# First products by slices of 2, 2, 4, 4, 4 blocks with six more pairs of partial sums, and six attention gates put into DRAM early

## The chip, the cores and the metric

The kernel runs on one core of one Trainium2 chip. The metric is the device time of one execution in microseconds. Three runs of the kernel before gave a median of 1566.24 us (1565.78 to 1566.56).

## The reference

One decoder block on x (256 tokens, width 2048, float32), conditioned on a vector c. What matters here:

```
mod = silu(c) @ w_ada + b_ada                      # 2048 x 12288: sh1, sc1, gt1, sh2, sc2, gt2
h = rms_norm(x, norm1_gain) * (1 + sc1) + sh1
p = h @ w_in + b_in                                # columns: r, k, v, LoRA inputs, q, ak, av, gates of both branches
y_rwkv = rwkv7_branch(p_rwkv, ...)                 # 16 heads of 64, a recurrence over the 256 tokens
y_attn = sliding_window_sink_attention(q, k, v, sinks)
merged = g_rwkv * (y_rwkv @ w_branch_rwkv) + g_attn * (y_attn @ w_branch_attn)
x = x + gt1 * (merged @ w_out)
x = x + gt2 * (relu(h2 @ w_up)**2 @ w_down)        # h2: rms_norm and sh2, sc2 again
return rms_norm(x, final_gain)
```

All weights are float32 and are read once. Products are made in three passes with a high and a low part of either operand.

## The kernel before

**Products.** A product keeps 128 x 128 blocks of weights as the stationary operand and streams the 256 tokens. `split` (L267) loads a piece of 1024 columns of weights (0.5 MB, tag `raw`, a ring of 7 buffers that the tiles of w_ada share), casts it to the high part on ScalarE (L274) and subtracts it for the low part on VectorE (L275). `feed` (L278) turns a piece into 24 products on TensorE (L297): high weights with high and low tokens, low weights with high tokens. `cols_product` (L303) is a product over the whole depth into one PSUM bank.

**Modulation and slices.** The first norm needs sh1 and sc1 for each block of 128 of the 2048 inputs. `modulated(part)` (L373) makes them for one slice of blocks (`SL`, L34): for the first slice with TensorE (`ada_pe`, L192), for the others with VectorE (`ada_dve`, L207, multiply-adds at L219). The loop at L948 goes over the slices. In each one it feeds the six kept banks (L955), which gather over all slices in PSUM (LoRA inputs, first keys, r, v, q, attention keys), and then the `sums` (L426): ten banks of 256 columns, two at a time, whose partial sums are taken out of PSUM after each slice, copied in the first one (L967) and added in SBUF in the others (L969). While a slice is fed, the modulation of the next one runs as a background job. In the last slice, after the fourth of the sums, `begin_heads` (L878) and `begin_attention` (L895) start the two branches.

**The order of the work.** Background jobs are generators. `pulse` (L253) is called after each piece and lets each queue take as many steps as its rate allows: `RATE_ADA` and `RATE_BG` for the rows of w_ada (`bg`), `RATE_ATT` for attention, `RATE_RW` for the RWKV branch. A step costs 1 credit, or what it yields: the steps of `chains` yield 0.5. The tile layer then orders the instructions on each engine and sets the waits; each engine works its list off in order, and SyncE issues nearly all DMAs, also in order.

**The RWKV branch** (`rwkv`, L771) works on four groups of heads, two at a time: `prep` (L480: decay, norm of the keys with the sums at L515, an inverse root on VectorE at L519 and its transposed copy at L537, and the triangular products at L566), `inverse16` (L608: the triangles go to DRAM at L573, are read back in another layout at L611, inverted in 30 steps on GpSimd at L619 and L621, written at L622 and L624 and read back at L629), `levels` (L636, from L644: the inverse is built up), `chains` (L675: the recurrence) and `norm` (L726). The second pair of groups needs the keys, r and v of `keyed` (L1002), which are products of their own at L1012; they go through DRAM.

**After the first products** come three gate products, the keys of the third group, those of the fourth, `gd2` (L996) and more gates. A gate of the RWKV branch is written to DRAM (`grd`) until it is used. Attention's gates are made just ahead of the branch product that uses them (L1029, L1032). `finish(rw)` at L1036 drains the RWKV branch before its own branch product (L1044).

Of the kernel before, what the change touches and what calls it, by code (L numbers as in the profile page):

```python
# [18 lines left out]
P = 128  # L19
# [12 lines left out]
NSUM = 4  # L32
NZ = 3
SL = (4, 4, 4, 4)  # L34

RATE_ADA = 1.5
RATE_RW = 1.2
RATE_ATT = 1.0
RATE_BG = (0.9, 0.3, 0.4, 0.2)
# [43 lines left out]
def hybrid_block(ctx: ExitStack, tc, x, c, w_ada, b_ada, norm1_gain, w_in, b_in, rwkv_mix, rwkv_w0,  # L83
# [194 lines left out]
    def feed(w, k0, nk, cols, blocks, xh, xl, begin, end, tw=T):  # L278


        width = sum(m for _, _, m in blocks)

        def load(raw, a, m):
            o = 0
            for c0, n in cols:
                nc.sync.dma_start(raw[:, :, o:o + n],
                                  w.rearrange("(kc p) n -> p kc n", p=P)[:, k0 + a:k0 + a + m, c0:c0 + n])
                o += n

        for a, n, hi, lo in split(nk, width, load):  # L290
            for wt, xs in ((hi, (xh, xl)), (lo, (xh,))):
                for kk in range(n):
                    k = k0 + a + kk
                    o = 0
                    for ps, j, m in blocks:
                        for xx in xs:
                            TE.matmul(ps[0:m, j * tw:(j + 1) * tw], lhsT=wt[:, kk, o:o + m], rhs=xx(k),  # L297
                                      start=(k == begin and xx is xh and wt is hi and j == 0),
                                      stop=(k == end and wt is lo), skip_group_check=True)
                        o += m  # L300
            pulse(0.5)
# [114 lines left out]
    def flat(t, g=0):  # L416
# [9 lines left out]
    sums = [(("k", 1), O_K + 256), (("r", 1), O_R + 256), (("v", 1), O_V + 256)] + \  # L426
           [(("q", i), O_Q + 256 * i) for i in range(1, 4)] + \
# [4 lines left out]
    rest = [(t_s1, 0), (t_s1, 1), (t_s2, 0), (t_s2, 1)] + rest  # L432

# [12 lines left out]
    sgd2 = kd[0:32, 0, :]  # L446
# [154 lines left out]
    def zero_inverses():  # L601
        z = arena[0][:, 2 * W3:2 * W3 + BP // 2]
        G.memset(z, 0.0)
        for n in range(2):
            for h in range(2):
                nc.sync.dma_start(scr2[n].rearrange("u (q e) -> (u q) e", q=4)[:, h * BP // 2:(h + 1) * BP // 2], z)
# [68 lines left out]
    def chains(sts, dds):  # L675
# [13 lines left out]
        for c in range(NCH):  # L689
# [11 lines left out]
            yield 0.5  # L701
# [8 lines left out]
            yield 0.5  # L710
# [11 lines left out]
            yield 0.5  # L722
# [79 lines left out]

    arena = [tl("a1", (8 * T,)), tl("a2", (8 * T,))]
# [67 lines left out]
    def pair(q2, qT=None):  # L871
        if qT is None:
            qT = qas[q2 % 2]
# [39 lines left out]
    for _ in range(8):  # L913
# [27 lines left out]
    def keys_out(ss, n, src):  # L941
# [4 lines left out]
        spilled.add((ss, n))  # L946

    for part, nk in enumerate(SL):  # L948
# [9 lines left out]
        for g2 in range(0, len(sums), 2):  # L958
            two = sums[g2:g2 + 2]
            ps = [ps_ax() for _ in two]  # L960
            feed(w_in, k0, nk, [(c, 256) for _, c in two], [(p, j, P) for p in ps for j in range(2)],
                 hA, hB, k0, k0 + nk - 1)
            for a, ((what, n), _) in enumerate(two):
                t, j = rest[g2 + a]
# [37 lines left out]
    def keyed(ss):  # L1002
        for n in range(3):
            keys_out(ss, n, cols_product(w_in, KC, (O_K, O_R, O_V)[n] + ss * 256, [P, P], hA, hB))
# [257 lines left out]
```

## Time and profile before

| | |
|---|---|
| median of 3 runs | 1566.24 us |
| profiled execution | 1566.93 us, span 1565.1 us |
| TensorE (PE) busy | 1510.9 us, 97% of the span |
| VectorE (DVE) busy | 1100.7 us, 70% |
| ScalarE (ACT) busy | 722.6 us, 46% |
| GpSimd (POOL) busy | 40.5 us, 3% |
| DMA | 372.8 MB, 238 GB/s on the mean |
| granted TensorE clock | 0.987 of full on the mean |

The profile is one execution, recorded by the hardware. Busy time is the union of an engine's instructions; TensorE's are pipelined, so the mean length of one product (286 ns) is longer than the distance to the next. Idle time in front of an instruction is shown in brackets with what ended it.

### The profile page before, as it was taken

The numbers are of one execution on the slowest core, as the hardware profiler recorded it, in microseconds if no ns is written. First come the engines' busy times: TensorE is split into PE (matmuls) and PEld (weight loads), VectorE is DVE, ScalarE is ACT, GpSimd is POOL, SyncE is SP. The second block draws the span as 40 slices with busy tenths as digits, with TensorE's granted clock in tenths as the row PEclk, the third lists the DMA queues.
The fourth block names the chain that finished last, engine by engine and source line by source line (L and its number), as shares of the span: only waits on it lengthen the run. The fifth ranks groups of instructions, "written<-read, shape, count | busy, mean of one in ns | idle before, by whom it ended". The sixth has DMA issues, their size and how long they took to land.

```text
span 1565.1 us, 30120 instructions
## 1 busy us (share of the span) xinstructions
PE 1510.9 (97%) x12122; PEld 1385.8 (89%) x12122; DVE 1100.7 (70%) x1784; ACT 722.6 (46%) x1107; POOL 40.5 (3%) x97
## 2 busy tenths in 40 slices
PE   5899999999999999999999999999999999999997
PEld 2898999889989898989889998989898898989985
DVE  1879979867789857669769755666666666555576
ACT  3353377655355433345447444434444343444443
POOL 2000000030000030000000000000000000000000
PEclk9899999999999999999999999999999999999999
DMA  9999978869888859849865777677776776566652
GB/s 343 335 325 295 342 234 245 245 170 310 283 262 285 269 155 297 282 147 339 285 215 173 240 222 228 216 222 226 225 228 211 227 222 205 184 188 189 194 183 81
DMA packets 297100, 372.80 MB, mean 238 GB/s; under 512 B 40912, under 2 KB 198384, under 8 KB 296320
## 3 DMA queue, kind: packets, MB, share of 16 engines
q1 hardware_dynamic: 296448, 370.72, 74.7%
q8 instruction: 95, 1.56, 0.4%
q0 software_dynamic: 512, 0.15, 0.1%
q14 instruction: 45, 0.37, 0.1%
HBM read 357.96 MB, written 12.86 MB: 237 GB/s over the span
## 4 chain that ended last, share of the span: by engine, by line
PE 87%; DVE 4%; DMA 3%; ACT 2%; issue 2%; POOL 1%; SPq 0%; POOLq 0%; DVEq 0%; ACTq 0%
PE mm L297 41%; PE mm L319 14%; PE ax L319 14%; PE ax L297 9%; PE ax L683 2%; PE ax L186 1%; PE ax L478 1%; DVE wlo L275 1%; DVE acc L219 1%; PE ax L566 1%; DMA ada<-in_w_ada_dram 1%; ACT whi L274 1%; DMA tt<-in_x_dram 1%; PE ax L653 0%; PE ax L237 0%
## 5 line engine op out<-in xcount | busy, mean ns | idle before, releaser
L274 ACT CAST whi<-raw 128x1024 fp32r<-128x1024 f32 x458 | 478.0, 1047 | 673.4 <-PE mm L297 257.0
L275 DVE TENSOR_TENSOR wlo<-raw,whi 128x1024 fp32r<-128x1024 f32 x458 | 557.0, 1219 | 267.3 <-ACT whi L274 258.6
L297 PE MATMUL mm<-h,whi 128*128 128x256 f32 (+1 forms) x3296 | 446.8, 286 | 3.4 <-ACT whi L274 3.4
L297 PEld LDWEIGHTS mm<-h,whi 128*128 128x128 f32 (+1 forms) x3296 | 415.2, 192 | 10.1 <-ACT whi L274 3.4
L219 DVE SCALAR_TENSOR_TENSOR acc<-ada,cact,acc 128x512 f32<-128x512 f32 x330 | 247.0, 749 | 60.2 <-DMA ada<-in_w_ada_dram 55.6
L297 PE MATMUL mm<-h,wlo 128*128 128x256 f32 (+1 forms) x1648 | 237.7, 284 | 0.0
L297 PEld LDWEIGHTS mm<-h,wlo 128*128 128x128 f32 (+1 forms) x1648 | 215.0, 191 | 1.1 <-issue 0.7
L319 PE MATMUL mm<-whi,u 128*128 128x512 f32 x512 | 138.3, 392 | 0.0
L319 PE MATMUL ax<-whi,u 128*128 128x512 f32 x512 | 138.0, 391 | 0.0
L297 PE MATMUL ax<-h,whi 128*128 128x256 f32 x768 | 109.0, 290 | 9.0 <-DVE p L969 4.5
L319 PEld LDWEIGHTS ax<-whi,u 128*128 128x128 f32 x512 | 96.2, 188 | 21.0
L319 PEld LDWEIGHTS mm<-whi,u 128*128 128x128 f32 x512 | 95.6, 188 | 20.2
L297 PEld LDWEIGHTS ax<-h,whi 128*128 128x128 f32 x768 | 100.2, 197 | 11.4 <-ACT whi L274 5.0
L319 PE MATMUL ax<-wlo,u 128*128 128x512 f32 x256 | 79.4, 391 | 0.0
L319 PE MATMUL mm<-wlo,u 128*128 128x512 f32 x256 | 79.3, 391 | 0.0
L297 PE MATMUL ax<-h,wlo 128*128 128x256 f32 x384 | 59.2, 287 | 0.0
L319 PEld LDWEIGHTS mm<-wlo,u 128*128 128x128 f32 x256 | 48.1, 188 | 10.5
L319 PEld LDWEIGHTS ax<-wlo,u 128*128 128x128 f32 x256 | 48.1, 188 | 10.5
L297 PEld LDWEIGHTS ax<-h,wlo 128*128 128x128 f32 x384 | 52.6, 197 | 0.1
L297 PE MATMUL mm<-tt,whi 128*128 128x256 f32 x256 | 37.7, 298 | 2.1 <-ACT tt L768 2.1
L297 PEld LDWEIGHTS mm<-tt,whi 128*128 128x128 f32 x256 | 34.5, 203 | 3.2 <-ACT tt L768 2.3
L319 PE MATMUL mm<-whi,m 128*128 128x512 f32 x128 | 35.0, 392 | 0.0
(345 smaller groups left out, 1489.1 us busy)
## 6 DMA issues: line engine op xcount, KB each, us to landing
ada<-in_w_ada_dram SPq DMA_DIRECT2D x192, 512.0 KB, 5.5
raw<-in_w_up_dram SPq DMA_DIRECT2D x128, 512.0 KB, 3.9
raw<-in_w_down_dram SPq DMA_DIRECT2D x128, 512.0 KB, 4.0
raw<-in_w_in_dram SPq DMA_DIRECT2D x72, 512.0 KB, 5.2
raw<-in_w_in_dram SPq DMA_DIRECT2D x128, 256.0 KB, 5.1
raw<-in_w_out_dram SPq DMA_DIRECT2D x32, 512.0 KB, 6.1
raw<-in_w_branch_attn_dram SPq DMA_DIRECT2D x16, 512.0 KB, 5.9
raw<-in_w_branch_rwkv_dram SPq DMA_DIRECT2D x16, 512.0 KB, 5.2
```

Source lines behind the costliest of these rows:

```text
L186: TE.matmul(ps[:, j:j + 1], lhsT=acc[:, j * P:(j + 1) * P], rhs=ones[:, 0:1], start=True, stop=True)
L219: V.scalar_tensor_tensor(o, in0=t[:, a, :], scalar=ck, in1=o, op0=ALU.mult, op1=ALU.add)
L274: S.copy(hi[:], raw[:])
L275: V.tensor_tensor(lo[:], raw[:], hi[:].bitcast(F32), op=ALU.subtract)
L297: TE.matmul(ps[0:m, j * tw:(j + 1) * tw], lhsT=wt[:, kk, o:o + m], rhs=xx(k), start=(k == begin and xx is xh and wt is hi and j == 0), sto ...
L319: TE.matmul(pss[tb][:], lhsT=uu(k)[:, sl], rhs=wt[:, kk, :], start=(first and k == 0), stop=(final and k == kblocks - 1))
L478: TE.matmul(out[hs, :], lhsT=src[hs, chunk(c)], rhs=ident[hs, hs], start=True, stop=True)
L566: TE.matmul(pT[hs, o:o + P], lhsT=src[hs, chunk(c)], rhs=ar[hs, i, c].rearrange("p a b -> p (a b)"), start=True, stop=True)
L683: TE.matmul(ps[hs, j, i, part, :], lhsT=lhs(j, i, hs), rhs=rhs(j, i, hs), start=(first and j == 0 and i == 0), stop=True, skip_group_check ...
```

## The change

The slices are 2, 2, 4, 4 and 4 blocks (`SL`), so the first products need the modulation of two blocks. The columns k, r and v of the third and fourth group of heads (`keys`) join the sums: 16 banks in place of ten; `keyed` is gone, and `keys_out` is called from the last slice. Four pairs, or one in a slice of 4 (`4 // nk`), are fed with one load of 0.5 MB, and with `apart` all products of one bank stand together. `begin_heads` is called after the third of the sums and `begin_attention` after the tenth, each with its own rate. The steps of `chains` cost 1 in place of 0.5, and the rates are 2.15 for RWKV (1.2 before), 1.35 for w_ada behind the first products (0.9) and 1.0 inside them (1.5). `gd2` and all RWKV gates follow the first products, then six attention gates, which go to DRAM (`grd` has 16 places), and two more are made where all eight were. In a slice of 2 blocks two pairs share a load.

```diff
-SL = (4, 4, 4, 4)
-
-RATE_ADA = 1.5
-RATE_RW = 1.2
+SL = (2, 2, 4, 4, 4)
+
+RATE_ADA = 1.0
+RATE_RW = 2.15
 RATE_ATT = 1.0
-RATE_BG = (0.9, 0.3, 0.4, 0.2)
+RATE_BG = (1.35, 0.3, 0.4, 0.2)
...
-    def feed(w, k0, nk, cols, blocks, xh, xl, begin, end, tw=T):
+    def feed(w, k0, nk, cols, blocks, xh, xl, begin, end, tw=T, apart=False):
...
+        groups = [[b for b in at if b[1] is ps] for _, ps, j, _ in at if j == 0] if apart else [at]
...
+            for group in groups:
+                for wt, xs in ((hi, (xh, xl)), (lo, (xh,))):
+                    for kk in range(n):
+                        k = k0 + a + kk
+                        for o, ps, j, m in group:
+                            for xx in xs:
+                                TE.matmul(ps[0:m, j * tw:(j + 1) * tw], lhsT=wt[:, kk, o:o + m], rhs=xx(k),
...
-    grd = tc.dram_tile([8, P, 2 * T], F32, name="grd")
+    grd = tc.dram_tile([16, P, 2 * T], F32, name="grd")
...
+    keys = [((n, ss), o + 256 * ss) for ss in (2, 3) for n, o in (("k", O_K), ("r", O_R), ("v", O_V))]
+    sums = [(("k", 1), O_K + 256), (("r", 1), O_R + 256), (("v", 1), O_V + 256)] + keys + [(("q", i), O_Q + 256 * i) for i in range(1, 4)] + \
            [(("g", g), O_GR + 256 * g) for g in range(NSUM)]
...
-    sgd2 = kd[0:32, 0, :]
+    sgd2 = mx.tile([32, T], F32, name="sgd2")
...
-            yield 0.5
+            yield
...
-                while len(spilled - {'gd2'}) < 7:
+                while not {w for w, _ in keys} <= spilled:
                     yield
...
-        for g2 in range(0, len(sums), 2):
-            two = sums[g2:g2 + 2]
-            ps = [ps_ax() for _ in two]
-            feed(w_in, k0, nk, [(c, 256) for _, c in two], [(p, j, P) for p in ps for j in range(2)],
-                 hA, hB, k0, k0 + nk - 1)
...
+        for g0 in range(0, len(sums), 4 // nk):
+            some = sums[g0:g0 + 4 // nk]
+            ps = [ps_ax() for _ in some]
+            feed(w_in, k0, nk, [(c, 256) for _, c in some], [(p, j, P) for p in ps for j in range(2)],
+                 hA, hB, k0, k0 + nk - 1, apart=True)
...
-            if last and g2 == 2:
-                finish(bg)
-                begin_heads()
-                begin_attention()
-                rate["rw"], rate["att"] = RATE_RW, RATE_ATT
+                    elif n > 1:
+                        keys_out(n, "krv".index(what), o)
+                    spilled.add((what, n))
+                    if (what, n) == ("v", 1):
+                        finish(bg)
+                        begin_heads()
+                        rate["rw"] = RATE_RW
+                    if (what, n) == ("q", 1):
+                        begin_attention()
+                        rate["att"] = RATE_ATT
...
+    def gates_late(g):
+        gate_out(8 + g, tl("gr", (2, T), 3), cols_product(w_in, KC, O_GA + g * 256, [P, P], hA, hB))
...
-    left = list(range(NSUM, 16))
-    for g in left[:3]:
+    gd2()
+    spilled.add("gd2")
+    for g in range(NSUM, 8):
         gates(g)
-    for ss in range(2, 4):
-        keyed(ss)
-        if ss == 3:
-            finish(att)
-            gd2()
-            spilled.add("gd2")
-    for g in left[3:8 - NSUM]:
-        gates(g)
+    for g in range(NLATE):
+        gates_late(g)
+    finish(att)
+    gates_late(NLATE)
...
-        gate_of(8 + g, t, cols_product(w_in, KC, O_GA + g * 256, [P, P], hA, hB))
+        if g <= NLATE:
+            nc.sync.dma_start(flat(t), grd[8 + g])
+        else:
+            gate_of(8 + g, t, cols_product(w_in, KC, O_GA + g * 256, [P, P], hA, hB))
```

Further, `zero_inverses` zeroes a smaller piece and writes it four times in place of twice, and the partial sums of the keys use the two attention tiles `a1` and `a2` before attention needs them.

Lines of the changed kernel that are named below: L303 is `feed`'s product (L297 before), L575 and L585 are in `prep` (L566, L576), L524 and L546 the norm of the keys (L515, L537), L653 the first product of `levels` (L644), L187 a column sum of w_ada (L186).

**The rates move the second inverse.** On TensorE, from the last triangular products of the second `prep` (L566) to the first products with the inverse (L644); `whi` is the high part of a piece of weights, `in` the inverse's data, `tt` the triangles. Each row of L297 below is the first one of a piece of 24 products. Before:

```order
L566 MATMUL ax_6819<-ar_6014,p_850_6520 64x128 x2
...
L297 MATMUL mm_7005<-a_719_5660,whi_7008 128x256
...
L297 MATMUL mm_7005<-a_719_5660,whi_7042 128x256
...
L297 MATMUL mm_7084<-h_218,whi_7087 128x256
...
L297 MATMUL mm_7084<-h_218,whi_7121 128x256
...
L297 MATMUL mm_7084<-h_219,whi_7196 128x256
...
L297 MATMUL mm_7084<-h_219,whi_7230 128x256
...
L297 MATMUL mm_7260<-a_719_5660,whi_7263 128x256
...
L297 MATMUL mm_7260<-a_719_5660,whi_7297 128x256
...
L297 MATMUL mm_7332<-h_218,whi_7335 128x256
...
L644 MATMUL ax_7375<-in_7074,tt_6286 64x64 x16
L644 MATMUL ax_7393<-in_7075,tt_6309 64x64 x16
```

And with the change:

```order
L575 MATMUL ax_6981<-ar_6334,p_898_6740 64x128 x2
...
L303 MATMUL mm_7161<-a_953_7133,whi_7164 128x256
L303 MATMUL mm_7287<-a_953_7133,whi_7290 128x256
...
L303 MATMUL mm_7161<-a_953_7133,whi_7251 128x256
...
L303 MATMUL mm_7287<-a_953_7133,whi_7324 128x256
...
L653 MATMUL ax_7360<-in_7123,tt_6544 64x64 x16
L653 MATMUL ax_7378<-in_7124,tt_6567 64x64
...
L653 MATMUL ax_7378<-in_7124,tt_6567 64x64 x15
```

Nine pieces of products stood between the two before, and four stand there now; the pieces with `a` are of the attention branch's product.

**The norm of the keys in the first pair of heads.** On TensorE, from the sums of squares (L515, into two `ax` banks) to the products with the inverse roots (`yn`, L537). Before, with the first rows of each piece and of the attention work between:

```order
L515 MATMUL ax_2767<-kt,p_358_2633 128x2 x2
L515 MATMUL ax_2794<-kt,p_367_2650 128x2 x2
L297 MATMUL ax_2828<-h_219,whi_2833 128x256
...
L297 MATMUL ax_2828<-h_219,whi_2864 128x256
...
L855 MATMUL ax_2893<-kt,a_50_248 128x128 x3
...
L297 MATMUL mm_2967<-h_218,whi_2970 128x256
...
L862 MATMUL ax_2892<-a_51_249,vtok 64x128
L864 MATMUL ax_2892<-a_51_249,vtok 64x128 x2
...
L855 MATMUL ax_2912<-kt,a_50_248 128x128 x3
...
L862 MATMUL ax_2911<-a_51_249,vtok 64x128
...
L537 MATMUL ax_2930<-kt,yn_2783 128x128 x2
L537 MATMUL ax_2944<-kt,yn_2810 128x128 x2
```

And with the change:

```order
L524 MATMUL ax_3239<-kt,p_435_3169 128x2 x2
L524 MATMUL ax_3266<-kt,p_444_3186 128x2 x2
L303 MATMUL ax_3301<-h_215,whi_3304 128x256
...
L303 MATMUL ax_3301<-h_215,wlo_3305 128x256 x8
L546 MATMUL ax_3332<-kt,yn_3255 128x128 x2
L546 MATMUL ax_3346<-kt,yn_3282 128x128 x2
```

One piece of 24 products is left in between; before there were more than two pieces and the steps of attention.

## Rows read from the trace of the kernel before

**Rows 1.** The page's busy times (busy, share of the span, instructions).

```profile
PE 1510.9 (97%) x12122; PEld 1385.8 (89%) x12122; DVE 1100.7 (70%) x1784; ACT 722.6 (46%) x1107; POOL 40.5 (3%) x97
```

**Rows 2.** TensorE's timeline at the start: begin, length (us), engine, line, what; idle before.

```profile
11.67 4.16 PE L200 MATMUL ax<-ada,in 128*32 128x512 f32 x12 [3.37 <-DMA ada<-in_w_ada_dram]
...
34.22 1.05 PE L200 MATMUL ax<-ada,in 128*32 128x512 f32 x4 [1.64 <-DMA ada<-in_w_ada_dram]
...
41.19 1.22 PE L297 MATMUL mm<-h,whi 128*128 128x256 f32 x4 [3.36 <-ACT whi L274]
```

**Rows 3.** A window of 50 us in the slices.

```profile
core 0: us, PE busy (x) PEld busy (x) DVE busy (x) ACT busy (x) POOL busy (x), PEclk, DMA share, GB/s
150.00:200.00 50.00, 47.42 (x391) 46.67 (x390) 46.50 (x64) 18.84 (x24) 0.00 (x0) 1.00 1.02 331
```

**Rows 4.** TensorE's timeline in the slices.

```profile
49.17 2.08 PE L297 MATMUL mm<-h,whi 128*128 128x256 f32 x16
51.09 1.12 PE L297 MATMUL mm<-h,wlo 128*128 128x256 f32 x8
...
132.20 0.95 PE L297 MATMUL ax<-h,whi 128*128 128x256 f32 x6 [1.35 <-DVE p L969]
...
139.20 1.05 PE L186 MATMUL ax<-kt,acc 128*128 128x1 f32 x8 [0.55 <-DVE tt L969]
...
190.60 1.05 PE L186 MATMUL ax<-kt,acc 128*128 128x1 f32 x8 [0.55 <-DVE tt L969]
```

**Rows 5.** VectorE by line, 100 to 200 us: busy, mean ns; idle before.

```profile
L219 DVE SCALAR_TENSOR_TENSOR acc<-ada,cact,acc 128x512 f32<-128x512 f32 x56 | 41.8, 749 | 1.0
L275 DVE TENSOR_TENSOR wlo<-raw,whi 128x1024 fp32r<-128x1024 f32 x32 | 38.6, 1219 | 1.2 <-ACT whi L274 1.1
...
L969 DVE TENSOR_TENSOR tt<-ax,tt 128x512 f32<-128x512 f32 x10 | 6.4, 686 | 0.9 <-PE ax L297 0.9
```

**Rows 6.** TensorE's timeline around the second inverse.

```profile
553.40 0.44 PE L566 MATMUL ax<-ar,p 64*64 64x128 f32 x4
...
586.64 0.30 PE L644 MATMUL ax<-in,tt 64*64 64x64 f32 x2 [0.80 <-DMA in<-scr]
589.12 1.99 PE L644 MATMUL ax<-in,tt 64*64 64x64 f32 x32 [2.19 <-DMA in<-scr]
592.26 1.97 PE L644 MATMUL ax<-in,tt 64*64 64x64 f32 x30 [1.15 <-DMA in<-scr]
```

**Rows 7.** SyncE's own queue at the second inverse.

```profile
554.61 1.25 SPq L573 DMA_DIRECT2D scr<-tt  x2
...
558.34 0.44 SPq L611 DMA_DIRECT2D lg<-scr  x1
...
582.24 7.43 SPq L629 DMA_DIRECT2D in<-scr  x8
```

**Rows 8.** GpSimd's timeline at both inverses.

```profile
346.06 0.63 POOL L623 COPY p<-p 128x256 f32<-128x256 f32 x1
...
563.53 0.47 POOL L619 TENSOR_TENSOR rs<-lg,p 128x15 f32<-128x15 f32 x1 [50.64 <-DMA lg<-scr]
...
579.16 0.63 POOL L623 COPY p<-p 128x256 f32<-128x256 f32 x1
```

**Rows 9.** TensorE's timeline around the first inverse.

```profile
319.22 0.44 PE L566 MATMUL ax<-ar,p 64*64 64x128 f32 x4
...
361.22 2.08 PE L644 MATMUL ax<-in,tt 64*64 64x64 f32 x64
```

**Rows 10.** TensorE's timeline at the last norm of the keys.

```profile
526.56 0.95 PE L515 MATMUL ax<-kt,p 128*128 128x2 f32 x8
...
539.79 0.71 PE L537 MATMUL ax<-kt,yn 128*128 128x128 f32 x4 [1.81 <-ACT yn L521]
```

**Rows 11.** Windows of 20 us behind two waits.

```profile
540.00:560.00 20.00, 20.00 (x241) 18.12 (x241) 15.87 (x32) 6.56 (x13) 0.00 (x0) 0.91 0.68 209
...
580.00:600.00 20.00, 15.86 (x214) 15.23 (x213) 8.59 (x13) 2.09 (x2) 0.00 (x0) 0.83 0.90 233
```

More of the change, by code (lines that the diff above doesn't have):

```diff
@@ L32 @@
 NSUM = 4
+NLATE = 5
 NZ = 3
-SL = (4, 4, 4, 4)
-RATE_ADA = 1.5
-RATE_RW = 1.2
+SL = (2, 2, 4, 4, 4)
+RATE_ADA = 1.0
+RATE_RW = 2.15
 RATE_ATT = 1.0
-RATE_BG = (0.9, 0.3, 0.4, 0.2)
+RATE_BG = (1.35, 0.3, 0.4, 0.2)
 RATE_Z = 2.0
@@ L276, in split @@
             yield a, m, hi, lo
-    def feed(w, k0, nk, cols, blocks, xh, xl, begin, end, tw=T):
+    def feed(w, k0, nk, cols, blocks, xh, xl, begin, end, tw=T, apart=False):
         width = sum(m for _, _, m in blocks)
+        at, o = [], 0
+        for ps, j, m in blocks:
+            at.append((o, ps, j, m))
+            o += m
+        groups = [[b for b in at if b[1] is ps] for _, ps, j, _ in at if j == 0] if apart else [at]
         def load(raw, a, m):
@@ L290, in feed @@
         for a, n, hi, lo in split(nk, width, load):
[L291 to L300, printed above, removed]
+            for group in groups:
[5 more added lines that the diff above has]
+                                TE.matmul(ps[0:m, j * tw:(j + 1) * tw], lhsT=wt[:, kk, o:o + m], rhs=xx(k),
+                                          start=(k == begin and xx is xh and wt is hi and j == 0),
+                                          stop=(k == end and wt is lo), skip_group_check=True)
             pulse(0.5)
@@ L432, in hybrid_block @@
     rest = [(t_s1, 0), (t_s1, 1), (t_s2, 0), (t_s2, 1)] + rest
+    arena = [tl("a1", (8 * T,)), tl("a2", (8 * T,))]
+    rest[3:3] = [(arena[i // 4].rearrange("p (a b) -> p a b", b=T), i % 4) for i in range(len(keys) + 1)]
+    del rest[3 + len(keys) + 1]
     def shifted(dst, ps, m, j):
@@ L601, in zero_inverses @@
     def zero_inverses():
-        z = arena[0][:, 2 * W3:2 * W3 + BP // 2]
+        z = arena[1][:, 6 * T:6 * T + BP // 4]
         G.memset(z, 0.0)
         for n in range(2):
-            for h in range(2):
-                nc.sync.dma_start(scr2[n].rearrange("u (q e) -> (u q) e", q=4)[:, h * BP // 2:(h + 1) * BP // 2], z)
+            for h in range(4):
+                nc.sync.dma_start(scr2[n].rearrange("u (q e) -> (u q) e", q=4)[:, h * BP // 4:(h + 1) * BP // 4], z)
     def inverse16(dds):
@@ L709, in chains @@
                 terms(pB, 0, tok("kt"), tok("vt"))
-            yield 0.5
+            yield
             if c < NCH - 1:
@@ L721, in chains @@
             S.copy(y[:, :, :, c, :], pB[:, :, :, 1, :])
-            yield 0.5
+            yield
         for j in range(2):
@@ L801, in hybrid_block @@
     yad = tc.dram_tile([8, P, T], F32, name="yad")
-    arena = [tl("a1", (8 * T,)), tl("a2", (8 * T,))]
     def slot(a, o, n, shape):
@@ L872, in pair @@
         if qT is None:
+            while ("q", q2) not in spilled:
+                yield
             qT = qas[q2 % 2]
@@ L911, in begin_attention @@
             att.append(pair(q2, q0 if q2 == 0 else None))
-    for _ in range(8):
+    for _ in range(4):
         next(first)
@@ L945, in keys_out @@
         nc.sync.dma_start(rkvd[3 * (ss - 2) + n], flat(t))
-        spilled.add((ss, n))
     for part, nk in enumerate(SL):
@@ L957, in hybrid_block @@
                  hA, hB, 0, KC - 1)
-        for g2 in range(0, len(sums), 2):
-            two = sums[g2:g2 + 2]
-            ps = [ps_ax() for _ in two]
-            feed(w_in, k0, nk, [(c, 256) for _, c in two], [(p, j, P) for p in ps for j in range(2)],
-                 hA, hB, k0, k0 + nk - 1)
-            for a, ((what, n), _) in enumerate(two):
-                t, j = rest[g2 + a]
+        for g0 in range(0, len(sums), 4 // nk):
[3 more added lines that the diff above has]
+                 hA, hB, k0, k0 + nk - 1, apart=True)
+            for a, ((what, n), _) in enumerate(some):
+                t, j = rest[g0 + a]
                 o = flat(t, j)
```

5 lines of the change are left out of this document (removed).

## The prediction, made before the run

> **What bounds the kernel now.** I read the page's busy times first: TensorE works 97% of the span [rows 1]. So nothing that only moves work between VectorE, ScalarE and the DMA queues can bring much; what the change can win or lose is TensorE's idle time, about 54 us (span 1565.1 minus 1510.9), and time at the lower clock. Then I went through TensorE's timeline and noted each pause. There are four places.
>
> The first is the start. TensorE takes up the first loads of w_ada at 11.67 and the sixteenth at 34.22, and the first projection product comes at 41.19 [rows 2]. The second is the slices behind it, while VectorE computes the next slice's modulation. From 150 to 200 us DMA has a share of 1.02 at 331 GB/s, VectorE is busy 46.5 of 50 us and TensorE 47.4 [rows 3]: three limits nearly at once. One slice lasts 51.4 us (139.20 to 190.60) [rows 4]. Its 384 products take 46.1 us at 0.120 (16 of them from 49.17 to 51.09 [rows 4]), the two column sums about 2, and 3.3 us are waits, as the 1.35 us for an addition on VectorE [rows 4].
>
> The third is the RWKV branch's dependent chains, which run between pieces of other products. Before the second triangular inverse TensorE ends the last `prep` products at 553.84 and then has nine pieces of products to do; still it waits 0.80, 2.19 and 1.15 us for the inverse's data, until 592.26 [rows 6]. That is a latency of 33 us to the first pair and 38 to the last. The fourth is the end of the kernel, which the change does not reach.
>
> The sum is made against the profiled execution (1566.93 us, 1.8 above its span); the median of the runs is 1566.24, 0.7 lower, and I add the result to the median.
>
> **1. A first slice of 2 blocks.** Before the first product 8 loads of w_ada are needed in place of 16. Three loads take 4.16 us with a last use of 1.05 [rows 2], so they land every 1.55 us; over all sixteen it is 22.55/15 = 1.50. The eighth lands at 11.67 + 7 x 1.5 = 22.2. Behind the last one came 7.0 us (34.22 to 41.19), for four blocks; with two, about 6. That gives 28 us; TensorE's 32 transposes lie in the same stretch and I allow 1 us for them: 29.2. Gain **12** (10 to 13).
>
> **2. The other slices.** No product is added: 1152 of them lie in the first three slices before, and the total is the same, since the six pairs of key columns were products of their own later. Added are evictions: 5 slices of 16 banks in place of 4 of 10, of which the first slice's are copies on ScalarE (6 more) and the others additions on VectorE (64 in place of 30). 34 more additions of 0.686 us [rows 5] are 23 us of VectorE.
> A full slice of 4 now has 528 products, 63.4 us, and 2 us of sums. DMA carries 22 + 16 loads of 0.524 MB, 19.9 MB in 65.5 us or 304 GB/s, under the 331 seen. VectorE has 22 x 1.219 + 32 x 0.749 + 16 x 0.686 = 61.8 us [rows 5]. Both fit, barely: 0.5 us of waits per slice. The second short slice does not fit: 32 us of products and 2 of sums, but VectorE has 11 x 1.219 + 24.0 + 11.0 = 48.4 us, because the modulation for 4 blocks lies in it. The first short slice has slack (11 x 1.219 and halved multiply-adds, 12 to 24 us, beside 33), and VectorE works ahead of TensorE, so I take 7 us of waits (0 to 16). Against 10 us of waits in three slices before: **-2** (-9 to +8). One bank at a time costs nothing by itself: a group holds TensorE 24 x 0.120 = 2.9 us, the addition of the bank before takes 0.686; what covers it is VectorE's slack, and the 1.35 us wait [rows 4] is the price per eviction if that goes.
>
> **3. The second inverse, 9 pieces become 4.** The diff only shows rates (1.2 to 2.15, and a chain step that costs 1 in place of 0.5). The rows of TensorE's order show what they do: from the last `prep` product to the first product that needs the inverse there were nine pieces of 24 products, and now there are four. In between lie, whatever the rates are: two writes to DRAM from 554.61, the read back at 558.34, GpSimd's steps from 563.53 to 579.8, two writes, eight reads from 582.24 over 7.43 us [rows 7, 8]. The first 16 products of the inverse need the third read: they started at 589.12, 35 us after the last `prep` product [rows 6]. Four pieces are 11.5 us, with the small products behind `prep` about 16. TensorE issues in order, so it stands for 35 - 16 = 19 us and 1 more for the second half: 20 in place of 4.1. **+16** (11 to 19; the lower end is a round trip 5 us shorter, an estimate for engines that are emptier while TensorE stands). While SyncE waits for GpSimd, the weight loads behind it wait too; they return within the same stall.
>
> **4. The first inverse.** It had no wait: 319.22 to 361.22 [rows 9], with GpSimd done at 346.69 [rows 8]. Counted in products and attention steps, about 25 us now lie before the first product that needs it, and the data needs 33 to 35 (as in step 3). **+9** (3 to 12).
>
> **5. Norm of the keys.** Between the column sums of squares and the product with their reciprocal root lie eleven short VectorE steps, for two heads in turn, among the other VectorE work: 13.2 us (526.56 to 539.79), the last 1.81 waited [rows 10]. In the first pair 24 products now lie in between, 2.9 us, where the order had more than 60 and attention steps; in the other three pairs 44 to 63 products. First pair 2 to 10 us of wait, each other one 0 to 4: I take 5 + 5 less the 1.8 of before, **+8** (2 to 15).
>
> **6. Two PSUM banks shared.** Heads now begin after the third pair of sums, attention after the tenth. Until then two banks are kept, and the sums and `prep` share the other two. Some eight hand-overs of a bank at 0 to 1.35 us [rows 4]: **+3** (0 to 9).
>
> **7. The clock.** Around the pause at 586 to 592 the granted clock was 0.83 on the mean of 20 us, so part of them ran at 1.2 GHz and not 2.4: 3.4 us lost, and behind the one of 1.81 us 0.91, 1.8 lost [rows 11]. Two long pauses and some short ones more: **+5** (1 to 9).
>
> **8. At nothing:** the early gates. Six products of 16 blocks move ahead of the branch product, six writes and six reads of 256 KB are added: 3.1 MB, 10 us of DMA at 300 GB/s, beside a DMA share of 0.68 [rows 11]; without that cover it is at most 10 us. The copies of `sgd2` and the zeroing in four parts are small and hidden by products.
>
> Sum: -12 - 2 + 16 + 9 + 8 + 3 + 5 = **+27 us, 1593**.
>
> The DMA trips were taken from the rows: from the first write to GpSimd's start 8.9 us for two trips, and from GpSimd's last step to the last product's start 13.1 for two [rows 6, 7, 8]. The Trainium skill (DMA: Bandwidth & Descriptors, the table of the two cost components) gives about 2.0 us per transfer, plus bytes at 436 GB/s. By that page, with the issue times of the rows, the trips would be some 5 us shorter per inverse, and the sum 1583, as an estimate; the rows show the longer trips here, and I keep to them.
>
> **Rivals.**
> *Faster: the chains' latency follows the load.* The 13.2 us of step 5 and GpSimd's 16 us come from engines that share with full ones. When TensorE stands, VectorE's queue empties, and the chains finish sooner. It decides if the round trip of step 3 falls to about 25 us: +5, first inverse 0, norm +2, banks 0, clock +1; with slices at -9 the sum is -12 - 9 + 5 + 2 + 1 = -13, **1553**. For it: VectorE is busy for only 8.6 of the 20 us around the second inverse [rows 11]. Against: in those same 20 us the data still took 35 us. Chance 0.15.
> *No change:* losses of steps 3 to 7 at a third of what I take, gain as taken: 1566. Chance 0.06.
> *Slower still: VectorE bounds both short slices,* 12 us more of waits there, and its lag reaches the full ones: **1605**. For it: 48.4 against 34 us. Against: VectorE's lead. Chance 0.2.
> My forecast itself: 0.59, with its own range 1570 to 1614.
>
> **Numbers.** About 0.2% (3 us) can be told from no change. Slower 0.59 + 0.20 = 0.79, same 0.06, faster 0.15. The range 1557 to 1614 leaves out 0.12 below, most of the first rival, and 0.08 above.
>
> **What would show it.** The first projection product near 29 us; TensorE idle at both inverses, some 9 and 20 us, with the data from `scr` named; a wait for `yn` of 2 to 10 us in the first pair of heads; low clock behind each. The forecast is wrong if TensorE waits under 8 us at the second inverse, or if the first product does not come by 32.

## The result, and the profile after

The changed kernel takes 1602.01 us (median of 4 runs, 1598.87 to 1608.09), the kernel before beside it 1566.40. The ratio is 1.0236 (95% interval 1.0213 to 1.0258): slower, by 36 us where 27 were forecast, inside the range. The profiled execution took 1604.27 us, 1.8 above its span.

The page's busy times of the changed kernel, in the columns of [rows 1]:

```profile
PE 1521.4 (95%) x12122; PEld 1396.4 (87%) x12122; DVE 1135.0 (71%) x1851; ACT 725.7 (45%) x1115; POOL 39.4 (2%) x97
```

TensorE's idle time is 1602.5 - 1521.4 = 81.1 us, 54.2 before. To see where, I cut the span into windows of 1 us and took from each TensorE's idle time and its busy time times the share that the granted clock lacked ("half clock" below: what the level of 1.2 GHz cost). The cuts between stages are the same instructions in both kernels; as they fall on whole windows, an entry is good to about 0.5 us.

| stage | idle before | after | half clock before | after |
|---|---|---|---|---|
| to the first projection product | 19.9 | 16.4 | 1.0 | 0.0 |
| to the first sum of squares (norm of the keys) | 9.8 | 11.3 | 5.8 | 6.5 |
| to the first product with the first inverse | 3.9 | 18.1 | 0.0 | 2.7 |
| to the last triangles of the second pair | 3.6 | 0.9 | 1.7 | 1.7 |
| to the first w_out product | 6.4 | 23.9 | 6.1 | 13.9 |
| to the end | 10.6 | 10.6 | 0.0 | 0.0 |
| span less both | 1496.4 | 1496.6 | | |

The last line is the point of the table: all 37.4 us of longer span are idle time (+26.9) and half clock (+10.3). That the rest is equal is a balance. The 64 products of w_ada ahead of the first product are half as wide, 6.5 us of work in place of 13.3. Behind the first product the same count grew by 6.6 us: a product in front of a pause is counted at its full length, and there are 52 such pauses in place of 34 (about half of the 6.6, an estimate); eight column sums of w_ada moved behind it too, and the rest is spread thinly.

TensorE's timeline of the changed kernel, the waits that matter:

```profile
30.26 1.22 PE L303 MATMUL mm<-h,whi 128*128 128x256 f32 x4 [2.37 <-ACT whi L275]
...
94.94 2.38 PE L303 MATMUL ax<-h,whi 128*128 128x256 f32 x16 [0.81 <-DVE a L978]
...
105.54 1.87 PE L187 MATMUL ax<-kt,acc 128*128 128x1 f32 x8 [1.84 <-DVE tt L978]
...
291.42 2.07 PE L546 MATMUL ax<-kt,yn 128*128 128x128 f32 x8 [4.35 <-ACT yn L530]
...
408.57 0.47 PE L653 MATMUL ax<-in,tt 64*64 64x64 f32 x2 [9.96 <-DVE a L829]
...
580.23 4.03 PE L303 MATMUL mm<-a,whi 128*128 128x256 f32 x17 [2.37 <-ACT a L1035]
...
603.59 0.47 PE L653 MATMUL ax<-in,tt 64*64 64x64 f32 x2 [9.26 <-DMA in<-scr]
605.49 2.27 PE L653 MATMUL ax<-in,tt 64*64 64x64 f32 x32 [1.43 <-DMA in<-scr]
```

The first line answers to the last of [rows 2]: the first product came 10.9 us earlier. The second and third lie in the second short slice, where VectorE's additions release TensorE. Then the norm, 4.35 us where the first pair had no such wait, and the inverses: 9.96 where [rows 9] had none, 10.7 where [rows 6] had 4.1.

Windows of the changed kernel: the second short slice, the stretch around the first inverse, and two around the second, to be read against [rows 11]:

```profile
core 0: us, PE busy (x) PEld busy (x) DVE busy (x) ACT busy (x) POOL busy (x), PEclk, DMA share, GB/s
60.70:107.40 46.70, 39.44 (x281) 36.70 (x281) 41.61 (x60) 16.27 (x21) 0.00 (x0) 0.94 0.96 314
400.00:414.00 14.00, 5.43 (x50) 5.11 (x51) 5.83 (x17) 2.06 (x11) 0.13 (x2) 0.63 1.10 222
578.00:590.00 12.00, 9.77 (x60) 9.78 (x61) 10.52 (x19) 4.68 (x10) 6.95 (x14) 0.72 0.81 229
596.00:614.00 18.00, 8.13 (x128) 7.55 (x128) 4.42 (x7) 0.00 (x0) 1.01 (x3) 0.53 0.90 222
```

The granted clock of 0.53 to 0.72 stands behind each long wait; around the second inverse TensorE ran nearly all the time at 1.2 GHz, the lower of its two levels.

The timeline of all engines at the first inverse shows why TensorE's row at 408.57 names VectorE and not the inverse's data:

```profile
387.13 0.46 SPq L142 DMA_DIRECT2D ada<-in_w_ada_dram  x1
...
399.39 0.37 SPq L631 DMA_DIRECT2D scr<-p  x1
...
402.05 0.39 SPq L142 DMA_DIRECT2D ada<-in_w_ada_dram  x1
402.54 6.03 SPq L638 DMA_DIRECT2D in<-scr  x8
406.51 1.54 DVE L220 SCALAR_TENSOR_TENSOR acc<-ada,cact,acc 128x512 f32<-128x512 f32 x2 [11.01 <-DMA ada<-in_w_ada_dram]
407.97 1.94 DVE L829 SCALAR_TENSOR_TENSOR a<-kt,ax 128x384 f32<-128x384 f32 x4
```

SyncE issues nothing from 387.6 to 399.4: its next transfer is the inverse's write, which waits for GpSimd. Behind it in the same queue stands a load of w_ada. VectorE waits 11 us for that load, and behind that multiply-add stands the step that empties attention's PSUM banks (L829). TensorE needs those banks. So a wait for GpSimd reaches TensorE through SyncE's and VectorE's queues, besides the inverse's own data, which came at the same time: the first of the eight reads took 4.7 us from 402.54 to its landing at 407.2, the third landed at 408.7.

SyncE's stop is not new. Its queue in the kernel before, at both inverses:

```profile
332.06 0.37 SPq L141 DMA_DIRECT2D ada<-in_w_ada_dram  x1
346.02 0.37 SPq L622 DMA_DIRECT2D scr<-p  x1
...
567.11 0.37 SPq L286 DMA_DIRECT2D raw<-in_w_in_dram  x1
579.12 0.37 SPq L622 DMA_DIRECT2D scr<-p  x1
```

It stood 13.6 and 11.6 us there, and 11.8 and 9.7 with the change. But between the last triangles and the first product with the inverse TensorE had 39.4 and 32.0 us of work (idle time and half clock taken off), and now has 25.2 and 16.2. The first products with the inverse waited 0 and 4.1 us there. So the stop by itself cost little; it costs where the work beside it runs out.

### The profile page after: what moved, and what is told of

It reads as the page before. It is cut to its first block, busy times and chain, and to the rows that moved or that the text cites. A ratio compares the mean times of both kernels' runs of the same rounds, so it can differ in the third digit from the quotient of the medians.

```text
span 1602.5 us, 30201 instructions
## 1 busy us (share of the span) xinstructions
PE 1521.4 (95%) x12122; PEld 1396.4 (87%) x12122; DVE 1135.0 (71%) x1851; ACT 725.7 (45%) x1115; POOL 39.4 (2%) x97
## 4 chain that ended last, share of the span: by engine, by line
PE 80%; DVE 8%; issue 4%; DMA 4%; POOL 2%; ACT 1%; SPq 0%; POOLq 0%; DVEq 0%; ACTq 0%
PE mm L303 34%; PE mm L324 14%; PE ax L324 13%; PE ax L303 10%; DVE acc L220 2%; DVE wlo L276 2%; DMA ada<-in_w_ada_dram 1%; PE ax L692 1%; PE ax L187 1%; DMA raw<-in_w_branch_attn_dram 1%; PE ax L487 1%; POOL p L630 1%; POOL rs L628 1%; PE ax L662 1%; PE ax L575 1%
## 5 line engine op out<-in xcount | busy, mean ns | idle before, releaser
L275 ACT CAST whi<-raw 128x1024 fp32r<-128x1024 f32 (+1 forms) x458 | 478.5, 1047 | 614.6 <-PE ax L324 222.1
L276 DVE TENSOR_TENSOR wlo<-raw,whi 128x1024 fp32r<-128x1024 f32 (+1 forms) x458 | 557.3, 1218 | 256.2 <-ACT whi L275 253.5
L303 PE MATMUL mm<-h,whi 128*128 128x256 f32 (+1 forms) x2912 | 396.0, 286 | 5.6 <-ACT whi L275 5.6
L303 PEld LDWEIGHTS mm<-h,whi 128*128 128x128 f32 (+1 forms) x2912 | 366.7, 192 | 12.1 <-ACT whi L275 6.2
L220 DVE SCALAR_TENSOR_TENSOR acc<-ada,cact,acc 128x512 f32<-128x512 f32 (+1 forms) x360 | 261.1, 726 | 60.8 <-DMA ada<-in_w_ada_dram 55.9
L303 PE MATMUL mm<-h,wlo 128*128 128x256 f32 (+1 forms) x1456 | 212.4, 284 | 1.0 <-DVE wlo L276 1.0
L303 PEld LDWEIGHTS mm<-h,wlo 128*128 128x128 f32 (+1 forms) x1456 | 190.0, 191 | 3.0 <-DVE wlo L276 1.2
L303 PE MATMUL ax<-h,whi 128*128 128x256 f32 x1152 | 163.4, 291 | 5.7 <-DVE sc L189 1.7
L303 PEld LDWEIGHTS ax<-h,whi 128*128 128x128 f32 x1152 | 151.0, 198 | 8.8 <-issue 3.4
L303 PE MATMUL ax<-h,wlo 128*128 128x256 f32 x576 | 87.8, 285 | 2.7 <-DVE wlo L276 2.7
L303 PEld LDWEIGHTS ax<-h,wlo 128*128 128x128 f32 x576 | 77.5, 193 | 3.5 <-DVE wlo L276 3.5
L303 PE MATMUL mm<-a,whi 128*128 128x256 f32 x256 | 37.6, 301 | 5.5 <-ACT whi L275 3.1
L303 PEld LDWEIGHTS mm<-a,whi 128*128 128x128 f32 x256 | 34.1, 205 | 7.2 <-ACT whi L275 3.5
L324 PE MATMUL ax<-whi,m 128*128 128x512 f32 x128 | 35.3, 394 | 0.0
```

Of the source, the lines that this page charges most:

```text
L220: V.scalar_tensor_tensor(o, in0=t[:, a, :], scalar=ck, in1=o, op0=ALU.mult, op1=ALU.add)
L275: S.copy(hi[:], raw[:])
L276: V.tensor_tensor(lo[:], raw[:], hi[:].bitcast(F32), op=ALU.subtract)
L324: TE.matmul(pss[tb][:], lhsT=uu(k)[:, sl], rhs=wt[:, kk, :], start=(first and k == 0), stop=(final and k == kblocks - 1))
```

## The experiments

Theory A is the prediction's: the order puts too little work behind the RWKV branch's serial steps. B puts the loss into slices and sums, C into the early gates. D came up on the way: what stands behind SyncE's wait for GpSimd. Ratios are to the kernel before on the same chip, with their intervals; idle time and half clock are of the profiled run, as above.

| run | ratio | idle | half clock |
|---|---|---|---|
| the kernel before | 1 | 54 | 15 |
| the changed kernel | 1.0236 (1.0213 to 1.0258) | 81 | 25 |
| rates alone | 1.0229 (1.0198 to 1.0260) | 80 | 22 |
| without GpSimd's steps | 1.0097 (1.0066 to 1.0128) | 60 | 11 |
| slices of 4 | 1.0177 (1.0157 to 1.0197) | 74 | 15 |
| short slices alone | 1.0051 (1.0029 to 1.0072) | 60 | 16 |
| gates late | 1.0264 (1.0243 to 1.0284) | 81 | 25 |
| more steps | 1.0199 (1.0179 to 1.0220) | 82 | 14 |
| steps ahead of the write | 1.0116 (1.0096 to 1.0136) | 67 | 20 |
| filler | 1.0221 (1.0202 to 1.0239) | 72 | 15 |
| combined | 1.0221 (1.0179 to 1.0263) | 80 | 26 |
| combined, steps ahead | 1.0118 (1.0097 to 1.0139) | 68 | 16 |
| before, steps ahead | 0.9971 (0.9954 to 0.9988) | 54 | 10 |
| before, one bank at a time | 1.0094 (1.0070 to 1.0118) | 59 | 28 |

**Rates alone, in the kernel before.**

```diff
-RATE_RW = 1.2
+RATE_RW = 2.15
-RATE_BG = (0.9, 0.3, 0.4, 0.2)
+RATE_BG = (1.35, 0.3, 0.4, 0.2)
...
-            yield 0.5
+            yield
```

> The kernel before with only the rates of the change: 2.15 for RWKV, chain steps at 1, 1.35 for w_ada behind the first products; slices, sums and gates stay. On TensorE 19 and 18.5 us of work then stand between the triangular products and the inverse (35 and 30 before), 5 to 9 at the norms. Theory A (the order alone makes the loss): some 13 us of waiting at each inverse, 2 at the first norm, 5 of half clock: 1594 where the kernel before has 1566, a ratio of 1.018 (1.010 to 1.026). Theory B (the loss comes with the sums and the slices): ratio 1.000 to 1.004.

Measured 1.0229, inside theory A's range and the same as the whole change. TensorE's timeline of this run:

```profile
342.84 0.44 PE L644 MATMUL ax<-in,tt 64*64 64x64 f32 x2 [11.70 <-DVE m L836]
...
494.75 3.78 PE L297 MATMUL mm<-h,whi 128*128 128x256 f32 x16 [3.13 <-ACT whi L274]
...
580.83 0.44 PE L644 MATMUL ax<-in,tt 64*64 64x64 f32 x2 [11.15 <-DMA in<-scr]
```

Three rates are enough for both inverse waits: 34.4 and 33.7 us pass from the last triangles to the first product with the inverse, and 22.7 and 21.4 of work fill them. Theory B falls as the main cause. Which of the three rates does it was not tried, nor the changed kernel with the old rates. What came beyond the forecast are waits for weights, seven of 0.3 to 3.1 us between 463 and 567, as at 494.75.

**Without GpSimd's steps.**

```diff
-        for s in range(15):
+        for s in range(1):
```

> Leaves out 28 of the 30 GpSimd steps of each triangular inverse, so this part of the computation is not done; everything else stands as in the changed kernel. Theory A (order: too few products stand behind the serial steps of the RWKV branch): the inverse's data come about 14 us sooner (the steps took 16 us in either kernel), the 10.0 and 10.7 us of waiting at the two first products with the inverse go, and so does the half clock behind them (some 5 us): 1576, range 1570 to 1584. Theory B (the loss is made in the slices, by short slices and 34 more additions on VectorE): the RWKV waits are slack that comes back as waits a few steps later, 1595 to 1602.

Measured 1.0097, by the ratios 22 us under the changed kernel, as theory A has it. SyncE's stops at the inverses shrank to 0.3 and 1.8 us. The wait at the first inverse and the two for `scr` are gone from its timeline, and half clock fell from 25 to 11. The waits of the norm stayed. So the first inverse's wait hangs on GpSimd too, although its row names VectorE.

**Slices of 4, and short slices alone.** The changed kernel with one constant back (and the eight tiles of its first slice taken up ahead of the transposes, as before), and the kernel before with that constant changed the other way:

```diff
-SL = (2, 2, 4, 4, 4)
+SL = (4, 4, 4, 4)
```

> The changed kernel with slices of 4, 4, 4, 4 blocks as before. Theory A: the first projection product comes at 41 in place of 30 us (+11), and the 7 us of waits and 2.5 us of half clock in the second short slice go (-9): 1604, range 1598 to 1610, and the waits of the RWKV branch stay as they are. Theory B: the short slices are the loss, so about 1575.

> The kernel before with only the slices of 2, 2, 4, 4, 4 blocks; ten banks in the sums, rates as they were. First product at 30 us (-11). In the second short slice VectorE has 41 us of work beside 25 us of TensorE, against 48 beside 34 in the changed kernel, where 7 us of waits and 2.5 of half clock came of it. If short slices cost what VectorE lacks: +10 to +13, so 1562 to 1570 where the kernel before has 1566. If the early start is worth its 11 us: 1555.

Slices of 4 gave 1.0177, 0.6% under the changed kernel, between the two theories and outside what either gave (1591.0 us). The first product came 9.5 us later (39.71), and still the branch was reached 8 us earlier. The windows of that run over the slices:

```profile
39.70:200.00 160.30, 158.90 (x1307) 158.68 (x1308) 140.30 (x178) 72.59 (x88) 0.00 (x0) 0.99 0.98 325
200.00:275.00 75.00, 74.14 (x603) 72.45 (x602) 58.36 (x89) 44.21 (x80) 0.21 (x2) 1.00 0.80 238
```

TensorE idles 2.3 us in 235 and loses 2.1 to half clock; the kernel before lost 9.8 and 5.8 there, the changed one 11.3 and 6.5. So two parts of the change work against each other: the sums as changed save 11 us against before, and the short slices bring 13 us back. That the key columns do it, by giving each slice enough products to hide VectorE, is argued: the run also feeds one bank at a time (a load holds the columns of two banks in a slice of 2 blocks, of one in a slice of 4) and has w_ada's rate of 1.0. In the last run below, one bank at a time left 9.9 us of idle time in this stage, and half clock there was 1.7 us. Short slices in the kernel before, where fewer products stand beside them, cost 0.5% (1573.1 us, above the 1562 to 1570 expected) although the first product came at 31.16: its stretch from 62 to 108 us idles 10.0 and loses 6.3 to half clock.

**Gates late.**

```diff
-NLATE = 5
+NLATE = -1
...
-    for g in range(NLATE):
-        gates_late(g)
     finish(att)
-    gates_late(NLATE)
```

> The changed kernel with all eight attention gates made where they were before, none through DRAM. Theory A: the same products stand behind the two inverses up to 2 us, so 1600, range 1596 to 1604. Theory C (the early gates are not free: 12 us more of waits and half clock lie behind 612 us, around the attention branch's product): 1588 to 1593, with fewer waits for weights behind 612 us.

1.0264 against 1.0236, with intervals that overlap: no cost of the early gates shows, and theory C is out.

**More steps, and where they stand.** Twelve empty steps behind the inverse's reads instead of three, one more at the norm, chain steps at 0.5, `RATE_RW` 2.6; then the same with eight of the twelve moved ahead of the write:

```diff
         for s in range(15):
...
+        for _ in range(8):
+            yield
         nc.sync.dma_start(blocks16(scr2[0]), x16[:, 0])
...
-        for _ in range(12):
+        for _ in range(4):
             yield
```

> The changed kernel with more empty steps in the RWKV branch: 12 in place of 3 behind the inverse, one more behind the norm of the keys, chain steps at 0.5 again, rate 2.6. On TensorE 34 and 28 us of work then stand between the triangular products and the inverse (21 and 14 with the change), and 5.8 in place of 2.9 us at the first norm. Theory A: the waits at the inverses go from 21 to 5 us, their half clock by 5, the norm by 2, and the denser chains give 5 back: 1583, range 1575 to 1592. Theory B: no change, 1598 to 1606.

> The run with more empty steps, with 8 of the 12 put ahead of the two writes that wait for GpSimd (4 stay behind the reads). On TensorE the same amount of work stands before the inverses (34 and 28 us); on SyncE the loads of the pieces between now stand ahead of the waiting write and not behind it. Theory D (SyncE stands 12 to 15 us for GpSimd, and the loads of weights and w_ada queued behind it make TensorE wait): the four waits of 5.9, 15.4, 5.6 and 3.7 us and 5 us of half clock go, up to 5 us of waiting for the inverse remains: 1568 where the kernel before has 1566, a ratio of 1.001 (0.996 to 1.008). Theory A (only the distance from the triangles to the inverse on TensorE counts): ratio 1.018 to 1.022 as in that run.

With more steps the waits for the inverse went, as theory A says, but only 0.4% of the time: 1.0199, between the two theories, with half clock at 14 in place of 25 and idle time still 82. In their place TensorE waited for attention's result. SyncE's own queue of that run:

```profile
564.46 0.50 SPq L142 DMA_DIRECT2D ada<-in_w_ada_dram  x1
579.60 0.37 SPq L632 DMA_DIRECT2D scr<-p  x1
...
588.85 1.65 SPq L1034 DMA_DIRECT2D gr<-yad  x3
```

and TensorE:

```profile
585.84 0.58 PE L303 MATMUL mm<-a,whi 128*128 128x256 f32 x1 [15.38 <-ACT a L1036]
```

SyncE stood 14.6 us, and the reads of attention's output (`yad`), which had nothing to do with the inverse, came behind it, the first of them at 582.18. With eight steps ahead of the write, SyncE's queue of the next run reads:

```profile
569.52 1.04 SPq L1036 DMA_DIRECT2D gr<-yad  x2
...
576.68 0.36 SPq L1036 DMA_DIRECT2D gr<-yad  x1
...
590.86 0.37 SPq L634 DMA_DIRECT2D scr<-p  x1
```

The reads stand ahead of the write; the wait at that product fell to 2.2 us, and by the ratios 13 us of the time went (1.0116). That supports D, at half the size I gave it and outside its range. The steps took away only one of the two stops: at the second inverse it fell from 14.7 to 0.1 us, at the first it stayed (11.1 and 11.0). There 6.1 us of waiting remain, with attention's step on VectorE still named, and waits of 2.5 to 3.5 us for weights and w_ada remain around the branch product.

**Filler.** 64 products into an unused bank in front of either inverse:

```diff
         for _ in range(3):
             yield
+        ps = ps_ax()
+        for _ in range(64):
+            TE.matmul(ps[:, 0:T], lhsT=hA(0)[:, 0:P], rhs=hA(1), start=True, stop=True)
```

> The changed kernel with 64 further products of 128x256 (7.7 us at full clock) on TensorE in front of the first product with either inverse, into a bank that nobody reads. They fit into the 10 us that TensorE waits there. If the low clock behind the inverses comes from those waits, it goes (1.7 us behind the first, 4 to 5 behind the second) and the rest stands: 1596 where the changed kernel has 1602. If the clock falls for another reason: 1602, and where the wait is shorter than the filling, up to 1612.

No difference to the changed kernel in time. Half clock fell by 9 us and idle by 9, and the rest of the span grew by 17: the filling cost what it saved. At the second inverse a wait of 8.8 us stood behind it. At the first inverse it waited itself:

```profile
409.89 9.50 PE L644 MATMUL ax<-h 128*128 128x256 f32 x64 [9.59 <-DVE a L832]
```

These products need nothing of the inverse, only a bank. So attention's banks alone hold TensorE there as long as the inverse's data do. For the clock: from the second triangles to 800 us half clock fell from 14.0 to 1.9 and idle time from 23.9 to 11.9. The time is that of the second expectation, but not for its reason: most of the low clock there did go, and the filling took what it gave.

**Combined, twice.** Slices of 4, no gates in the sums, attention's output read three gates earlier, `RATE_RW` 1.8, chain steps 0.5, two more steps at the norm, 8 behind the inverse; then 6 ahead of the write and 3 behind the reads.

```diff
-SL = (2, 2, 4, 4, 4)
+SL = (4, 4, 4, 4)
-NSUM = 4
+NSUM = 0
-RATE_RW = 2.15
+RATE_RW = 1.8
...
```

> A version made of the parts: the changed kernel with slices of 4 blocks; the gates of the RWKV branch all behind the sums (none in the sums), so that more work stands beside the branch; rate 1.8, chain steps 0.5, 8 empty steps behind the inverse and two more behind the norm (42 and 34 us of work before the inverses, 9 to 10 at the norms); attention's results are read three gates earlier, ahead of the inverse's waits on SyncE. Theory A: from the run with slices of 4 the waits at inverses and norms (26 us) and 8 us of half clock go: 1553, range 1545 to 1563, where the kernel before has 1566. Theory B: as the run with slices of 4, 1590.

> The combined version with 6 of its 9 steps ahead of the writes that wait for GpSimd, 3 behind the reads. Theory D: the seven waits there for weights, w_ada and what hangs on them (36 us) and some 12 us of half clock go: 1556, range 1548 to 1566, a ratio to the kernel before of 0.989 to 1.000. Theory A: no change against that run, 1600 to 1606.

Both missed, by 50 and 27 us. On TensorE's order the first had more work before the inverses than the kernel before (42 and 34 us against 35 and 30, counted on the order), and it waited 8.6 and 7.9 us for w_ada's multiply-adds and 7.7 and 3.9 for weights instead. SyncE stood 10.4 and 9.0 us for GpSimd there, 5.0 and 0.1 with the steps moved. Distance on TensorE did not help here while the loads for it stood behind that stop. Moving the steps took 16 us away by the ratios, 21 by the medians (the first version's runs lie from 1591.5 to 1606.0). What held the second version is not settled: its timeline has ten waits of 0.6 to 5.0 us between 571 and 631, most of them for weights, where SyncE also stands before the writes of the branch product (`mad`).

**The kernel before, with steps ahead of the write, and then one bank at a time.** Three steps ahead of the write, two behind the reads, rate 1.3; then the ten sums one pair at a time, one more step at the norm, rate 1.35.

```diff
-RATE_RW = 1.2
+RATE_RW = 1.3
...
+        for _ in range(3):
+            yield
         nc.sync.dma_start(blocks16(scr2[0]), x16[:, 0])
...
-        for _ in range(3):
+        for _ in range(2):
             yield
```

> The kernel before with 3 steps ahead of the writes and 2 behind the reads (before: 3 behind), rate 1.3 for RWKV. 41 and 35 us of work stand before the inverses (35 and 30 before). Theory D and A both: the waits of 4.1 us at the second inverse and 2.7 us of half clock behind it go, the norm of the second pair (5.8 us of work in place of 9.9) costs up to 2: ratio 0.997 (0.994 to 1.000).

> The last run (the kernel before with steps ahead of the writes) with the ten sums fed one pair of columns at a time, as the change does, one more empty step at the norm of the keys and rate 1.35; 42 and 35 us of work stand before the inverses, 9 to 11 at the norms. The slices still lose 9.9 us of waits and 6.3 of half clock in that run. Theory E (those waits are the hand-over of a bank from VectorE to TensorE): at 0.6 to 1.4 us each they go, about 6 us with the clock: ratio to the kernel before 0.993 (0.989 to 0.996). Theory F (VectorE has 50 us of work for 48.5 of TensorE in each slice, and one bank at a time changes nothing in that): the waits come back at other places, ratio 0.997 to 0.999.

The first is the fastest of all and beats both kernels: 0.9971 of the kernel before (0.9954 to 0.9988), as expected: the inverse's waits are gone from its timeline (its first product with the second inverse, at 588.12, waits for nothing). It does not speak for D: SyncE still stood 11.1 and 11.8 us at the inverses. More work stands in front of the inverses (46.2 and 37.8 us for 39.4 and 32.0), as theory A asks. Idle time as a whole did not fall (54); half clock did, by 4 us. The second fell short of both theories, 1.0094. Idle time hardly moved (59 against 54; the waits in the slices turned from additions to `wlo`, 0.7 to 1.5 us each, as theory F has it), but half clock rose from 10 to 28 us. The windows with most of it:

```profile
457.00:475.00 18.00, 17.43 (x97) 13.62 (x97) 10.60 (x46) 9.26 (x22) 0.00 (x0) 0.62 0.64 204
678.00:706.00 28.00, 27.64 (x140) 19.81 (x141) 11.76 (x53) 11.89 (x30) 0.00 (x0) 0.54 0.15 45
```

TensorE is busy for 27.6 of 28 us at a granted clock of 0.54, behind a wait of 5.2 us. Both stretches hold the branch's last step, small products of 64 rows and pairs of 128x256 (L478, L757, L758) between pieces of weights. The kernel before ran the same products behind the second pair (L478, L754, L755) with no wait among them:

```profile
678.00:694.00 16.00, 16.00 (x135) 11.60 (x133) 9.80 (x38) 9.79 (x24) 0.00 (x0) 1.00 0.43 138
694.00:700.00 6.00, 6.00 (x40) 6.00 (x40) 2.72 (x6) 1.03 (x4) 0.00 (x0) 0.72 0.19 51
```

They ran at full clock there, and then it fell although TensorE had been busy without a break. So no wait was needed for the clock to fall, and these products can run at the upper level. That they keep it down once a wait has lowered it fits both traces but was not tried.

## Why the prediction was right

The sign and the main cause were right: the rates, which in the diff are numbers, cost the time through the order. By its steps:

1. **First slice, -12:** the first product came 10.9 us earlier. But idle time fell by 3.5 only, and half clock by 1.0. The other 6.5 us are work (20.4 us ahead of the first product, 13.9 now), above all w_ada's products at half the width. By the table it is lost again behind the first product, where the count of work grew by 6.6.
2. **Other slices, -2:** +2.2 (idle and half clock to the first sum of squares). Inside its bounds, with the other sign, and small for a reason that I had not split: -11 by the sums, +13 by the short slices. The estimate of 7 us of waits in the second short slice was right (7.3), but 2.5 of half clock there and 4.0 in its neighbours were not in the step.
3. **Second inverse, +16:** +6.6 (10.7 in place of 4.1). The place and the releaser were as said; the size, under its lower end of 11, failed at "35 - 16 = 19". The work was as counted, 16.2 us. From the last triangles to the products that need the third read it was 33.0 us, not 35.3. Of the 16.8 us between, the inverse's waits are 10.7; the rest are other waits in front (2.6) and half clock (3.1), the wait for `a` at 580.23 and the clock of 0.72 above. The trips were about 2 us shorter: 8.0 us from the first write to GpSimd's start (8.9 before), 8.9 from its last step to the third read's landing (9.9 before; the 13.1 of the prediction goes on to a later read). The sentence beside it, by which they would be some 5 us shorter (the Trainium skill, DMA: Bandwidth & Descriptors, the table of the two cost components), is not borne out by this trace.
4. **First inverse, +9:** 10.0, and the sum is borne out: 35.2 us from the last triangles to the first product, 25.2 of them work. But I had one of two paths. The wait also came through SyncE, w_ada, VectorE and attention's banks. "While SyncE waits for GpSimd, the weight loads behind it wait too; they return within the same stall" (step 3) held here to about 1 us, by the landings above; it failed in the run with more steps, where the reads behind the stop made TensorE wait 15.4 us.
5. **Norm of the keys, +8:** waits of 4.35, 0.96 and 0.51 us less the 1.8 of before, +4.0, inside its bounds. The first pair was the one, as said.
6. **Two banks, +3:** at most 2.3, four waits of 0.15 to 1.55 us for VectorE or ScalarE between 277 and 338.
7. **The clock, +5:** +10.3, above its upper end of 9. Most of it, 7.8, lies in the stage of the second inverse (13.9 us against 6.1). My 3.4 us around the pause before counted idle time in; by busy time (15.86 us at 0.83) it is 2.7.
8. **Early gates, 0:** nothing, by the run with late gates.

What was not foreseen: in the stage behind the second pair's triangles idle time rose by 17.5 us, and the inverse is 6.6 of it. The rest are waits for attention's output and for weights (2.4 at 580.23, 2.2 at 619.77, 3.2 at 694.01, 1.0 at 697.18) and shorter ones in the levels. The two runs with steps ahead of the write (1.0199 to 1.0116, and 1.0221 to 1.0118) show that SyncE's stop has a part in such waits once there are more steps; how large a part it has in the changed kernel itself was not measured.

That the sum came within 10 us of the result is in part luck. Steps 3 and 5 were 13 us too high together, and against them stand 5 us in step 7, 4 in step 2 and the 11 us of waits that no step had.

*The rival "faster"* needed a round trip of 25 us when TensorE stands. From the end of the last triangles at 572.5, the second one fell from 32.8 to 31.1 us to the first product, and from 35.3 to 33.0 to those that need the third read; the first was 35.2. If there is such an effect, it is far too small.

The Trainium skill (DMA: Bandwidth & Descriptors, under the fixed cost) says that a wait for a semaphore happens on the sequencer that issues, before it hands the transfer on. The rows at 564.46 and 579.60 agree: SyncE issued nothing for 14.6 us, and the reads of `yad` came only behind it.

## What to carry to other kernels

A rate or priority in a scheduler is a change of order: list what stands between a serial chain's last step and its first user, on the waiting engine and on the queue that feeds it, and compare both with the chain's latency. A transfer that waits for a slow engine belongs late in its queue, behind the loads that the time in between needs. In the changed kernel, adding work on TensorE without moving the transfer moved most of the wait to another place (1.0236 to 1.0199); in the kernel before, with more work beside it, a stop of the same length cost little. A shorter first stage pays only if its neighbours can still hide their own preparation.

## What the hardware showed that I had not expected

A wait on one queue reached TensorE through two other engines: 11.8 us of SyncE became 11.0 of VectorE and 10.0 of TensorE. Behind a stop of 13.6 us at the same place of the kernel before, the first product with the inverse did not wait. The half clock was over a quarter of the loss (10.3 of 37.4 us), and in one run it was 0.54 on the mean of 28 us in which TensorE was busy 99% of the time. In the kernel before it fell at 694 us without any wait in the 16 us ahead.
